# The first load of a rotary-embedding kernel in two pieces (16 and 112 partitions), and ScalarE copies of two PSUM banks each

## Chip, cores, metric

One core of a Trainium2 chip. The metric is the device time of one execution in microseconds (us). Most executions of one kernel agree within 0.3%; some, of any kernel, fall in a slower state and are left out of comparisons. Ratios below are the mean time of one kernel's fast runs over that of the other's fast runs of the same rounds, so they are not quite the ratio of the medians quoted beside them. Where some runs of a kernel fell in the slower state (the changed kernel, e1, e4, e5, e11), the median of its fast runs is given too; the ratio is what counts. Bytes and packet lengths come from one profiled fast run of each kernel.

## The reference

```python
# x: (8, 2048, 8, 64) f32; cos, sin: (2048, 32) f32
x1, x2 = x[..., :32], x[..., 32:]
out1 = x1 * cos - x2 * sin          # cos, sin broadcast over batch and heads
out2 = x1 * sin + x2 * cos
return np.concatenate([out1, out2], axis=-1)
```

It reads 33.6 MB of x and 0.5 MB of tables and writes 33.6 MB.

## The kernel before

The sequence lies on 128 partitions, 16 rows of it on each, so one batch is a tile of 128 x 8192 f32 (4 MB), loaded by the sync engine and stored by ScalarE's queue out of the same tile. GpSimd (POOL) makes the products with sin, VectorE (DVE) those with cos, and one of three ways adds them: "A" on VectorE; "B" on TensorE, which adds through an identity matrix into PSUM, from where ScalarE copies; "C" likewise, with both products on VectorE. Five units of 2048 columns go through TensorE, the first of batches 1 to 5.

```python
    o_pool = ctx.enter_context(tc.tile_pool(name="op", bufs=2, space=PSUM))
    ...
    def load(b):
        xt = xpool.tile([P, ROW], f32, tag="xt", name=f"xt{b}")
        for lo, n in spans([UNIT, UNIT, 2 * UNIT] if b == 0 else [ROW]):   # UNIT = 2048 columns
            keep(nc.sync.dma_start(out=xt[:, lo : lo + n], in_=xv[b, :, lo : lo + n]))
            if b == 0 and lo == 0:
                keep(nc.sync.dma_start(out=cos_sb, in_=cos_src))
                keep(nc.sync.dma_start(out=sin_sb, in_=sin_src))
    ...
        elif kind == "B":
            for j in range(n // C):                                        # C = 512, one bank
                o = o_pool.tile([P, C], f32, tag="o")
                cs = slice(j * C, (j + 1) * C)
                nc.tensor.matmul(o, eye, t1[:, cs], start=True, stop=False)
                nc.tensor.matmul(o, eye, t2[:, cs], start=False, stop=True)
                keep(nc.scalar.copy(xt[:, cs], o))
    ...
    def shares(b):                # columns of each store
        if b == 0:
            return [HD, 7 * HD, 2 * UNIT]                                  # HD = 512
        if b == last:
            return [2 * UNIT, UNIT, UNIT]
        return [ROW]
```

## Time and profile before

| | kernel before |
|---|---|
| time, median of 3 (then of 6) | 163.72 us (163.66) |
| span of the profiled run | 161.4 us |
| DMA share of the span | 98.2% |
| DVE, POOL, PE, ACT busy | 87%, 86%, 29%, 9% |

### The profile page before, as it was taken

Reading aid. Unit: us, or ns where it says so; the run is one execution under the profiler, and the core shown is the slowest. Engines: PE = TensorE matmul, PEld = TensorE weight load, DVE = VectorE, ACT = ScalarE, POOL = GpSimd, SP = SyncE. Lnnn points to the kernel's source line nnn. Section 1 sums busy time; section 2 is a strip of 40 time slices with the busy share of each in tenths; the row PEclk is TensorE's granted clock in tenths of the full one; section 3 lists DMA queues with packets and bytes.
Section 4 is the critical chain, followed back from the end, with each engine's and each line's share of the span. In section 5 each row is a group of like instructions: output and inputs, shape, how many; then the busy total and the mean of one; then the engine's idle time right before and its main releaser. Section 6 shows DMA issues by size and latency. Waiting matters only on the chain.

```text
span 161.4 us, 467 instructions
## 1 busy us (share of the span) xinstructions
PE 46.4 (29%) x80; PEld 18.5 (11%) x80; DVE 140.1 (87%) x66; ACT 14.4 (9%) x24; POOL 139.0 (86%) x70
## 2 busy tenths in 40 slices
PE   0000000498008960893029912980000000000000
PEld 0000000133003420340014401430000000000000
DVE  0468899999999999999999999999899998999900
ACT  3200000013000220032001210140000000000000
POOL 1299999999999899998996999998999979999200
PEclk9999999999955696599755985799555555555555
DMA  5999999899999999999999999999999999999995
GB/s 181 418 445 464 449 430 390 373 427 499 406 390 447 430 487 390 447 438 414 447 422 430 447 416 438 447 406 447 455 392 455 447 398 455 438 406 455 410 398 231
DMA packets 3458, 67.65 MB, mean 419 GB/s; under 512 B 384, under 2 KB 384, under 8 KB 768
## 3 DMA queue, kind: packets, MB, share of 16 engines
q1 hardware_dynamic: 1728, 34.08, 49.8%
q10 hardware_dynamic: 1728, 33.56, 48.4%
q14 instruction: 2, 0.02, 0.0%
HBM read 34.08 MB, written 33.55 MB: 419 GB/s over the span
## 4 chain that ended last, share of the span: by engine, by line
DMA 46%; DVE 37%; POOL 9%; issue 2%; SPq 1%; DVEq 0%; POOLq 0%; ACTq 0%
DMA xt<-in_x_dram 24%; DVE t L128 18%; DMA out_dram<-xt 18%; DVE xt L135 17%; POOL t L121 9%; DMA sin_sb<-in_sin_dram 3%; DVE t L145 1%; SPq L69 0%; SPq L67 0%; DVEq L135 0%; POOLq L121 0%; ACTq L74 0%
## 5 line engine op out<-in xcount | busy, mean ns | idle before, releaser
L121 POOL TENSOR_TENSOR t<-xt,sin_sb 128x1024 f32<-128x1024 f32 (+1 forms) x32 | 70.4, 2200 | 10.7 <-DMA sin_sb<-in_sin_dram 5.7
L128 DVE TENSOR_TENSOR t<-xt,cos_ps 128x2048 f32<-128x2048 f32 (+1 forms) x34 | 73.4, 2166 | 0.8
L121 POOL TENSOR_TENSOR t<-xt,nsin 128x1024 f32<-128x1024 f32 (+1 forms) x32 | 70.4, 2200 | 0.0
L135 DVE TENSOR_TENSOR xt<-t,t 128x2048 f32<-128x2048 f32 (+1 forms) x29 | 62.2, 2144 | 6.2 <-POOL t L121 3.7
L140 PE MATMUL o<-t,eye 128*128 128x512 f32 x24 | 17.1, 803 | 25.2 <-DVE t L128 25.2
L156 PE MATMUL o<-t,eye 128*128 128x512 f32 x16 | 10.9, 781 | 36.8 <-DVE t L128 36.8
L141 PE MATMUL o<-t,eye 128*128 128x512 f32 x24 | 15.0, 710 | 0.0
L142 ACT COPY xt<-o 128x512 f32<-128x512 f32 x12 | 7.0, 586 | 46.5 <-PE o L141 46.5
L140 PEld LDWEIGHTS o<-t,eye 128*128 128x128 f32 x24 | 5.6, 247 | 33.5 <-issue 33.5
L161 ACT COPY xt<-o 128x512 f32<-128x512 f32 x8 | 4.7, 586 | 42.6 <-PE o L157 42.6
L156 PEld LDWEIGHTS o<-t,eye 128*128 128x128 f32 x16 | 3.6, 247 | 41.7 <-POOL t L121 30.6
L141 PEld LDWEIGHTS o<-t,eye 128*128 128x128 f32 x24 | 5.9, 248 | 8.5 <-issue 8.5
L92 DVE COPY cos_ps<-cos_sb 128x512 f32<-128x512 f32 x1 | 0.7, 695 | 6.2 <-DMA cos_sb<-in_cos_dram 6.2
L157 PE MATMUL o<-t,neye 128*128 128x512 f32 x8 | 4.9, 714 | 0.2 <-DVE t L145 0.2
L145 DVE TENSOR_TENSOR t<-xt,sin_ps 128x2048 f32<-128x2048 f32 x2 | 4.6, 2279 | 0.0
L157 PE MATMUL o<-t,eye 128*128 128x512 f32 x8 | 4.1, 592 | 0.0
L157 PEld LDWEIGHTS o<-t,neye 128*128 128x128 f32 x8 | 1.8, 239 | 3.6 <-issue 3.6
L157 PEld LDWEIGHTS o<-t,eye 128*128 128x128 f32 x8 | 1.5, 190 | 1.9 <-issue 1.9
L89 ACT ACT_TABLE_LOAD x1 | 1.3, 1283 | 0.7 <-PEq L204 0.7
L89 ACT ACTIVATE nsin<-sin_sb 128x512 f32<-128x512 f32 x1 | 0.6, 629 | 4.9 <-DMA sin_sb<-in_sin_dram 4.9
L90 ACT COPY sin_ps<-sin_sb 128x512 f32<-128x512 f32 x1 | 0.6, 580 | 0.0
L79 POOL MEMSET eye<- 128x128 f32 x1 | 0.2, 205 | 0.3 <-POOLq L204 0.3
(6 smaller groups left out, 1.0 us busy)
## 6 DMA issues: line engine op xcount, KB each, us to landing
xt<-in_x_dram SPq DMA_DIRECT2D x7, 4096.0 KB, 38.9
out_dram<-xt ACTq DMA_DIRECT2D x6, 4096.0 KB, 28.3
out_dram<-xt ACTq DMA_DIRECT2D x2, 2048.0 KB, 18.9
xt<-in_x_dram SPq DMA_DIRECT2D x2, 1024.0 KB, 6.0
xt<-in_x_dram SPq DMA_DIRECT2D x1, 2048.0 KB, 11.5
out_dram<-xt ACTq DMA_DIRECT2D x2, 1024.0 KB, 8.7
out_dram<-xt ACTq DMA_DIRECT2D x1, 1792.0 KB, 20.4
cos_sb<-in_cos_dram SPq DMA_DIRECT2D x1, 256.0 KB, 5.0
```

The costliest lines, as they stand in the source:

```text
L89: keep(nc.scalar.mul(nsin, sin_sb, -1.0))
L92: keep(nc.vector.tensor_copy(cos_ps, cos_sb))
L121: nc.gpsimd.tensor_mul(out=t2u[:, :, u, :].rearrange("p (r h) d -> p r h d", h=H), in0=xu[:, :, 1 - u, :].rearrange("p (r h) d -> p r h d" ...
L128: nc.vector.tensor_mul(out=t1.rearrange("p (r k d) -> p r k d", r=nr, d=Dh), in0=xk, in1=rep(cos_ps[:, r0 : r0 + nr, :], 2 * H),)
L135: keep(nc.vector.tensor_add(out=xt, in0=t1, in1=t2))
L140: nc.tensor.matmul(o, eye, t1[:, cs], start=True, stop=False)
L141: nc.tensor.matmul(o, eye, t2[:, cs], start=False, stop=True)
L142: keep(nc.scalar.copy(xt[:, cs], o))
L145: nc.vector.tensor_mul(out=t2.rearrange("p (r k d) -> p r k d", r=nr, d=Dh), in0=xk, in1=rep(sin_ps[:, r0 : r0 + nr, :], 2 * H),)
L156: nc.tensor.matmul(o, eye, t1u[:, gs, u, :], start=True, stop=False)
L157: nc.tensor.matmul(o, eye if u else neye, t2u[:, gs, 1 - u, :], start=False, stop=True)
L161: nc.scalar.copy(xu[:, gs, u, :], o.rearrange("p (g d) -> p g d", d=Dh))
```

## The change

The intent: a small first load that gives each of the 16 DMA engines one row at once, so that all start early; and half as many ScalarE instructions. Cut to its core (the "C" branch is changed in the same way as "B"):

```diff
-    o_pool = ctx.enter_context(tc.tile_pool(name="op", bufs=2, space=PSUM))
+    o_pool = ctx.enter_context(tc.tile_pool(name="op", bufs=1, space=PSUM))
...
+    rows = {(0, 0): [slice(0, 16), slice(16, P)]}
...
-            keep(nc.sync.dma_start(out=xt[:, lo : lo + n], in_=xv[b, :, lo : lo + n]))
+            cs = slice(lo, lo + n)
+            for ps in rows.get((b, lo), [slice(0, P)]):
+                keep(nc.sync.dma_start(out=xt[ps, cs], in_=xv[b, ps, cs]))
...
-            for j in range(n // C):
-                o = o_pool.tile([P, C], f32, tag="o")
-                cs = slice(j * C, (j + 1) * C)
-                nc.tensor.matmul(o, eye, t1[:, cs], start=True, stop=False)
-                nc.tensor.matmul(o, eye, t2[:, cs], start=False, stop=True)
-                keep(nc.scalar.copy(xt[:, cs], o))
+            for j in range(n // (2 * C)):
+                o = o_pool.tile([P, 2 * C], f32, tag="o")
+                for k in range(2):
+                    cs = slice((2 * j + k) * C, (2 * j + k + 1) * C)
+                    oc = o[:, k * C : (k + 1) * C]
+                    nc.tensor.matmul(oc, eye, t1[:, cs], start=True, stop=False)
+                    nc.tensor.matmul(oc, eye, t2[:, cs], start=False, stop=True)
+                keep(nc.scalar.copy(xt[:, 2 * j * C : 2 * (j + 1) * C], o))
```

More of the change, by code (lines that the diff above doesn't have):

```diff
@@ L152, in rotate @@
             for u in range(2):
+                o = o_pool.tile([P, n // 2], f32, tag="o")
                 for j in range(n // 2 // C):
-                    o = o_pool.tile([P, C], f32, tag="o")
+                    oc = o[:, j * C : (j + 1) * C]
                     gs = slice(j * G, (j + 1) * G)
-                    nc.tensor.matmul(o, eye, t1u[:, gs, u, :], start=True, stop=False)
+                    nc.tensor.matmul(oc, eye, t1u[:, gs, u, :], start=True, stop=False)
                     nc.tensor.matmul(
-                        o, eye if u else neye, t2u[:, gs, 1 - u, :], start=False, stop=True
+                        oc, eye if u else neye, t2u[:, gs, 1 - u, :], start=False, stop=True
                     )
-                    keep(
-                        nc.scalar.copy(
-                            xu[:, gs, u, :], o.rearrange("p (g d) -> p g d", d=Dh)
-                        )
+                keep(
+                    nc.scalar.copy(
+                        xu[:, :, u, :], o.rearrange("p (g d) -> p g d", d=Dh)
                     )
+                )
     def pieces(b):
```

## The prediction

> **What bounds the kernel now.** I read the page first: engine shares, the DMA row over the 40 slices, the queues.
>
> ```profile
> PE 46.4 (29%) x80; PEld 18.5 (11%) x80; DVE 140.1 (87%) x66; ACT 14.4 (9%) x24; POOL 139.0 (86%) x70
> ...
> DMA  5999999899999999999999999999999999999995
> GB/s 181 418 445 464 449 430 390 373 427 499 406 390 447 430 487 390 447 438 414 447 422 430 447 416 438 447 406 447 455 392 455 447 398 455 438 406 455 410 398 231
> ...
> q1 hardware_dynamic: 1728, 34.08, 49.8%
> q10 hardware_dynamic: 1728, 33.56, 48.4%
> ```
>
> The two queues (loads, stores) together occupy 98.2% of the 16 DMA engines' span; DVE and POOL are near it with 87% and 86%, ScalarE is at 9%. So the first question is whether DMA or the DVE/POOL pair sets the end. Busy time by stretch (PE, PEld, DVE, ACT, POOL, then clock, DMA share, GB/s) shows where DMA is not full:
>
> ```profile
> 0.00:2.00 2.00, 0.00 (x0) 0.00 (x0) 0.00 (x0) 1.27 (x1) 0.70 (x6) 1.00 0.24 41
> 2.00:4.00 2.00, 0.00 (x0) 0.00 (x0) 0.00 (x0) 0.01 (x1) 0.00 (x0) 1.00 0.86 319
> 4.00:8.00 4.00, 0.00 (x0) 0.00 (x0) 1.76 (x2) 1.09 (x3) 0.97 (x1) 1.00 1.03 420
> 8.00:24.00 16.00, 0.00 (x0) 0.00 (x0) 13.44 (x9) 0.26 (x2) 16.00 (x10) 1.00 1.02 431
> ...
> 131.00:152.00 21.00, 0.00 (x0) 0.00 (x0) 19.79 (x11) 0.00 (x0) 18.60 (x10) 0.50 0.98 424
> 152.00:160.00 8.00, 0.00 (x0) 0.00 (x0) 1.23 (x1) 0.00 (x0) 0.00 (x0) 0.50 0.94 397
> ```
>
> Only the first 4 us are not full. By the packet records, 67.6 MB go between the first packet at 1.75 us and the end of the last at 160.25 us: 427 GB/s on average, 430 to 434 in nearly every stretch from 32 us on, whether it is load, store or a mixture. The time is therefore about 1.75 us of start, 158.5 us of full DMA, and 1.2 us until the program's end.
>
> Next, whether the end waits for DVE anyway. The last adds, and the issue of the last store (1 MB), stand in the order of time:
>
> ```profile
> 150.74 1.23 DVE L128 TENSOR_TENSOR t<-xt,cos_ps 128x1024 f32<-128x1024 f32 x1
> 152.07 1.23 DVE L135 TENSOR_TENSOR xt<-t,t 128x1024 f32<-128x1024 f32 x1
> ...
> 153.33 0.34 ACTq L74 DMA_DIRECT2D out_dram<-xt  x1
> ```
>
> That store lands at 160.6, 7.3 us later, although 1 MB is only 2.5 us of DMA: the store issued before it lands only at 158.2, so the last one starts moving at about 157.8. A store with a free queue would start about 1.0 us after its issue (the first load, below), at 154.3. So DVE could finish some 3 us later before it would delay the end. The chain of waits on the page names 37% DVE, but where it goes through the DMA (46%) it shows queueing; a shorter DVE would change nothing.
>
> **What the Trainium skill says.** "DMA: Bandwidth & Descriptors", section "Where 436 GB/s comes from", puts the ceiling of the 16 DMA engines' ports at 435.2 GB/s; the trace agrees, with 430 to 434. At that rate the 67.6 MB alone need 155.4 us (an estimate from that figure), so at most 3 us is to be had in the 158.5. The same page, "Latency and other measured facts", gives about 600 ns to the first byte of a DMA issued from sync; here the first issue ends at 1.11 us and the first packet starts at 1.75, 0.64 us later. Its section "Why a DMA increments its semaphore by 16 and not by 1" says that a copy runs on the largest number of engines up to 16 that divides its outermost size: 16 and 112 partitions both give 16, one row and seven rows per engine. "SBUF — State Buffer", section "Door 1: The DMA port swizzle", says that partitions 0 to 15 reach only 4 of the 16 memory-side ports and lists 104 GB/s for them at 1 MiB. No load of the kernel before has fewer than 128 partitions, so no run here shows that yet.
>
> **The change, part one: the split load.** The sync engine's issues now:
>
> ```profile
> 0.74 0.37 SPq L67 DMA_DIRECT2D xt<-in_x_dram  x1
> 1.16 0.43 SPq L69 DMA_DIRECT2D cos_sb<-in_cos_dram  x1
> 1.64 0.42 SPq L70 DMA_DIRECT2D sin_sb<-in_sin_dram  x1
> ```
>
> The spacing is 0.42 to 0.48 us. One more issue puts the cos, sin and all later loads some 0.45 us later in the sequencer. That alone costs nothing: cos would be issued at about 1.6 and queue behind 1 MB that moves until about 5 us. What can gain is the very first packets. By the packet records, the 16 engines' first packets (8 KB) start one after the other from 1.75 to 2.53 us, 2.03 on average, and take 0.39 to 1.09 us, against 0.309 us for an 8 KB packet later. If that stagger is the handing out of 8 rows to one engine after another, then 16 rows, one each, put all engines to work near 1.75; the 112 rows follow 0.42 us later, so the last engine gets them at about 2.53 + 0.42 - 0.1 = 2.85 us. That engine will by then have moved one packet; before, it had its first packet (0.58 us long) done at 3.11. Gain: about 0.25 us, and for the mean engine about 0.1 to 0.15 us. As DMA never idles again, it carries to the end nearly whole.
>
> Against it stands the port limit. 16 rows of 8 KB are 131 KB; at 104 GB/s (the skill's figure) they take 1.26 us, an estimate, where a full-width wave takes 0.31 us. Engines whose single row waits there until about 3.2 us would have moved one packet instead of the two and a half that they move now: a loss of up to 0.5 us on the slowest. In the 112-row load an engine's seven rows no longer lie on one port; I put collisions at 0 to 0.2 us. The sum of gain and loss runs from -0.25 to +0.7 us. I choose -0.1: first packets are slow now too (0.39 to 1.09 us), so part of the port wait lies inside that latency.
>
> **Part two: two banks per copy.** ScalarE's 20 copies of 512 columns take 0.586 us each, 11.7 us. Its two multiplications at the start (128 columns 0.299 us, 512 columns 0.629) give 0.86 ns per column, so 1024 columns should take 0.586 + 512 x 0.86 ns = 1.03 us; 10 of them are 10.3 us. ScalarE saves 1.4 us of work of which none is on a path. With one buffer of two banks in place of two of one bank, TensorE must wait for the copy between the halves of a unit, where it used to run on. Take the tightest case, the third batch:
>
> ```profile
> 57.44 0.59 ACT L142 COPY xt<-o 128x512 f32<-128x512 f32 x1 [1.13 <-PE o L141]
> 59.15 0.59 ACT L142 COPY xt<-o 128x512 f32<-128x512 f32 x1 [1.13 <-PE o L141]
> 63.05 0.34 ACTq L74 DMA_DIRECT2D out_dram<-xt  x1
> ```
>
> Copies come every 1.72 us, so one bank's matmuls take 1.72 us. The first double copy can start at 55.7 (where the second single copy started) and end at 56.75; two banks of matmuls end at about 60.3; the second double copy ends at about 61.4, against 59.74 now. The store is issued at 63.05, when DVE's last add is done: 1.6 us of slack left. Even with matmuls at the cold pace (0.86 us per pass, eight passes) the store slips under 2 us, and it would still queue behind the preceding store, which lands at 73.2. The buffers that TensorE holds longer (the operands t) are taken again later: the next batch's multiply into such a buffer starts at 62.88, and TensorE is done at 60.3. The built program keeps the same order on DVE, POOL, ScalarE and sync, with the waits on the same producers; TensorE loses half of its waits on ScalarE. Part two: 0.0 us.
>
> Sum: 163.72 - 0.1 + 0.0 = 163.6 us.
>
> **Rivals.** (1) The 16 rows crowd on four ports and the start is lost, not won: +0.3 to +0.7 us, 164.0 to 164.4. For it: the skill's table. Against it: it is 131 KB once. (2) The start gains more, because one slow engine carries its late start to the end: the last store's 16 completions are spread from 159.74 to 160.59, 0.85 us, about as wide as the stagger of 0.78 us at the start. If the stagger is what spreads the end, levelling it is worth up to 0.5 us: 163.2. (3) The serialised TensorE and ScalarE reach a path: it would need a slip of over 1.6 us and then a store queue that runs dry; the DMA row shows none, so 163.7 at most. (4) cos and sin land later, DVE starts later (now at 6.2 us) and takes the end: it needs 3 us, the extra issue is 0.45 us; 163.7.
>
> **Range and chances.** The three runs of before spread over 0.58 us, more than any single effect. I take -0.7 to +0.7 around the sum: 162.9 to 164.3. A change of 2% is 3.3 us, more than everything that the start and the end of the DMA stream hold together and could give (about 3 us) and four times the worst port loss. So within 2% has 0.98, and 0.01 for each side.
>
> **What would show it right or wrong.** In the changed kernel, DMA share 9 from the second slice on; the first packets of 16 engines all starting within about 0.2 us, near 1.75; their length tells the port question (0.4 to 0.9 us: no crowding; 1.2 us and over: rival 1). Ten ScalarE copies of 1.0 us; the third batch's last one ending near 61.4, before its store. DVE's last add within 0.5 us of 153.3. It would be wrong if DVE or POOL showed new waits for TensorE, if the stores were issued late enough for the DMA row to show a gap, or if the steady rate left 430 GB/s.

## More of the kernel before

What matters most for this change is the opening, in stretches of 2 us (length, PE, PEld, DVE, ACT, POOL busy with the number of instructions, then granted clock, DMA share, GB/s); kernel before:

```profile
2.00:4.00 2.00, 0.00 (x0) 0.00 (x0) 0.00 (x0) 0.01 (x1) 0.00 (x0) 1.00 0.86 319
4.00:6.00 2.00, 0.00 (x0) 0.00 (x0) 0.00 (x0) 0.00 (x0) 0.00 (x0) 1.00 0.97 385
6.00:8.00 2.00, 0.00 (x0) 0.00 (x0) 1.76 (x2) 1.09 (x3) 0.97 (x1) 1.00 1.09 455
8.00:10.00 2.00, 0.00 (x0) 0.00 (x0) 0.62 (x2) 0.26 (x2) 2.00 (x3) 1.00 1.07 455
```

DMA share and GB/s are two different things: the share counts the time that packets take, so an engine that waits inside a packet is "busy". Keep that in mind for the same lines after.

## The result, and the profile after

164.19 us median of 6 (164.03 to 169.16; fast runs 164.10) against 163.66 for the kernel before: ratio 1.0032, 95% interval 1.0017 to 1.0046. That is within 2%, and inside the range of the prediction, 0.1 us under its upper end; but the interval excludes 1, so the change costs about 0.5 us where the prediction had chosen a gain of 0.1.

The first profiled run fell in the slow state (169.16 us). There, 14 of the 16 completions of a late load came by 133.2 us and the last two at 137.5, some 4 us late, as if two DMA engines lagged; the last store ended in the same way, with 14 completions by 162.96 us and two at 166.48. The granted clock was no lower (0.768; 0.767 to 0.776 in this kernel's fast runs). The changed kernel was run again and profiled (e1 in the experiments, 164.17 us). Its page, answering to the prediction's first fence:

```profile
DMA  5999998989998999899899999999999999999994
GB/s 143 329 432 499 429 420 381 488 383 432 492 416 388 452 452 452 388 468 436 388 484 420 388 478 420 404 476 412 430 452 412 444 444 404 460 436 404 424 406 204
...
q1 hardware_dynamic: 1744, 34.08, 49.9%
q10 hardware_dynamic: 1728, 33.56, 48.1%
```

The queues hold 98.0% of the span, DMA is full from the second slice on, as before. Yet the first two slices moved 143 and 329 GB/s, where they moved 181 and 418. The opening of the same run:

```profile
2.00:4.00 2.00, 0.00 (x0) 0.00 (x0) 0.00 (x0) 0.01 (x1) 0.00 (x0) 1.00 0.92 234
4.00:6.00 2.00, 0.00 (x0) 0.00 (x0) 0.00 (x0) 0.00 (x0) 0.00 (x0) 1.00 0.99 284
6.00:8.00 2.00, 0.00 (x0) 0.00 (x0) 0.25 (x1) 0.00 (x0) 0.00 (x0) 1.00 1.07 372
8.00:10.00 2.00, 0.00 (x0) 0.00 (x0) 1.68 (x2) 1.35 (x3) 1.43 (x2) 1.00 1.12 467
```

Up to 6 us the share is as high as before, or higher, and the rate is a quarter lower; from 6 to 8 us it is still a fifth lower. The engines are at work all the time, on slower packets. After 8 us both run alike. The sync engine's issues and VectorE's first instruction, changed kernel:

```profile
0.74 0.83 SPq L70 DMA_DIRECT2D xt<-in_x_dram  x2
1.62 0.42 SPq L72 DMA_DIRECT2D cos_sb<-in_cos_dram  x1
...
7.75 0.69 DVE L95 COPY cos_ps<-cos_sb 128x512 f32<-128x512 f32 x1 [7.75 <-DMA cos_sb<-in_cos_dram]
```

cos is issued 0.46 us later than before and lands 1.55 us later (DVE starts at 7.75, where it started at 6.20), so 1.1 us of the delay is slower transfer. The end of the same run:

```profile
152.90 1.23 DVE L138 TENSOR_TENSOR xt<-t,t 128x1024 f32<-128x1024 f32 x1
...
154.15 0.34 ACTq L77 DMA_DIRECT2D out_dram<-xt  x1
```

VectorE ends 0.82 us later than before, not 1.55, because its waits for POOL and POOL's for x grew shorter. The last store is issued at 154.15 and lands at 161.48, while the store ahead of it lands only at 159.06: it still queues. DMA sets the end, as before. (The chain of waits on this page gives 75% to DVE and 4% to DMA, where the kernel before had 37% and 46%. It follows the last store back to its issue and from there to VectorE; how long that store then stood in its queue, it does not weigh. The two chains look like different bounds, and the bound is the same.)

### The profile page after: what moved, and what is told of

Same layout as the page of the kernel before. It is cut to its first block, busy times and chain, and to the rows that moved or that the text cites. A ratio compares the mean times of both kernels' runs of the same rounds, so it can differ in the third digit from the quotient of the medians.

```text
span 167.4 us, 461 instructions
## 1 busy us (share of the span) xinstructions
PE 48.8 (29%) x80; PEld 18.4 (11%) x80; DVE 140.1 (84%) x66; ACT 12.8 (8%) x14; POOL 139.0 (83%) x70
## 4 chain that ended last, share of the span: by engine, by line
DMA 47%; DVE 36%; POOL 8%; issue 2%; SPq 1%; DVEq 0%; POOLq 0%; ACTq 0%
DMA xt<-in_x_dram 25%; DMA out_dram<-xt 18%; DVE t L131 18%; DVE xt L138 17%; POOL t L124 8%; DMA sin_sb<-in_sin_dram 4%; DVE t L150 1%; SPq L70 0%; SPq L72 0%; DVEq L138 0%; POOLq L124 0%; ACTq L77 0%
## 5 line engine op out<-in xcount | busy, mean ns | idle before, releaser
L162 PE MATMUL o<-t,eye 128*128 128x512 f32 x16 | 11.9, 834 | 40.7 <-DVE t L131 38.5
L145 PE MATMUL o<-t,eye 128*128 128x512 f32 x24 | 16.7, 785 | 23.4 <-DVE t L131 19.9
L146 PE MATMUL o<-t,eye 128*128 128x512 f32 x24 | 14.9, 709 | 0.0
L147 ACT COPY xt<-o 128x1024 f32<-128x1024 f32 x6 | 6.1, 1012 | 45.7 <-PE o L146 45.7
L167 ACT COPY xt<-o 128x1024 f32<-128x1024 f32 x4 | 4.0, 1012 | 47.8 <-PE o L163 47.8
L163 PE MATMUL o<-t,neye 128*128 128x512 f32 x8 | 6.2, 863 | 0.2 <-DVE t L150 0.2
L163 PE MATMUL o<-t,eye 128*128 128x512 f32 x8 | 4.1, 592 | 0.0
```

The lines of the kernel that those rows point to most:

```text
L145: nc.tensor.matmul(oc, eye, t1[:, cs], start=True, stop=False)
L146: nc.tensor.matmul(oc, eye, t2[:, cs], start=False, stop=True)
L147: keep(nc.scalar.copy(xt[:, 2 * j * C : 2 * (j + 1) * C], o))
L162: nc.tensor.matmul(oc, eye, t1u[:, gs, u, :], start=True, stop=False)
L163: nc.tensor.matmul(oc, eye if u else neye, t2u[:, gs, 1 - u, :], start=False, stop=True)
L167: nc.scalar.copy(xu[:, :, u, :], o.rearrange("p (g d) -> p g d", d=Dh))
```

## The experiments

The tool for most of them is a count of bytes by time, from the start and length of every DMA packet in the trace (a packet is one row of a load on one DMA engine; its bytes are spread evenly over its length). MB moved since the start:

| kernel | 3 us | 4 us | 6 us | 8 us | 12 us | 24 us | 32 us | 64 us | last packet ends, us |
|---|---|---|---|---|---|---|---|---|---|
| before | 0.231 | 0.644 | 1.466 | 2.317 | 4.039 | 9.149 | 12.441 | 26.290 | 160.25 |
| changed (e1) | 0.215 | 0.498 | 1.087 | 1.796 | 3.496 | 8.666 | 12.123 | 25.969 | 161.14 |
| split only (e2) | 0.222 | 0.494 | 1.134 | 1.859 | 3.560 | 8.730 | 12.187 | 26.034 | 161.21 |
| banks only (e3) | 0.272 | 0.673 | 1.492 | 2.343 | 4.066 | 9.172 | 12.494 | 26.306 | 160.21 |
| column split (e4) | 0.225 | 0.565 | 1.361 | 2.191 | 3.912 | 9.040 | 12.339 | 26.177 | 160.77 |
| 112 first (e7) | 0.208 | 0.579 | 1.096 | 1.610 | 3.299 | 8.468 | 11.924 | 25.771 | 161.75 |
| 64 and 64 (e8) | 0.136 | 0.415 | 0.863 | 1.328 | 2.986 | 8.154 | 11.609 | 25.455 | 162.40 |

At 432 GB/s, 0.1 MB is 0.23 us. The changed kernel is 0.543 MB (1.26 us) behind at 12 us, and 0.318 MB (0.74 us) at 32 us: part is given back on the way. e1 and e2 have the same loads, so what lies between them, 0.15 us at 12 us, shows how far single traces differ.

Theories after the result. A: the shape of the loads costs; A1 in the 16 rows, A2 in the 112. B: one more DMA ahead of cos and sin costs, whatever its shape. C: the two-bank copies cost, since TensorE and ScalarE now take turns.

### e1 to e4: which part of the change

**e1_after_again**: the changed kernel, no edit.

> The changed kernel once more, for a profile of a fast run: the one at hand is of the slow state. All theories: 164.1 us, 0.3% over before. In the fast profile the opening should look as in the slow one: the 16 one-row packets take 0.3 to 0.5 us, the 112-row packets behind them 0.5 us and more, cos lands near 8.5 us instead of 6.2; and the end should be late by 0.5 to 0.8 us, with DMA full in between.

164.26 us median (fast runs 164.09 to 164.35) against 163.36; ratio 1.0036 (1.0010 to 1.0062). (The median of the four fast runs is 164.14.) The opening is slow in the expected way, though less than expected: cos is complete at 7.73 us, not 8.5, and the 8 KB packets between 3.5 and 5.5 us take 0.431 us. The last packet ends 0.89 us later.

**e2_split_only**: the kernel before with the `rows` lines of the diff alone.

> The split load alone, with the single-bank copies of before. Theory A (the shape of the 112-row load costs) and theory B (one more DMA ahead of cos and sin costs): all of the difference, +0.4 to +0.7 us over before. Theory C (the two-bank copies cost, through TensorE and ScalarE in turn): 0.0 us.

164.38 against 163.36; ratio 1.0052 (1.0029 to 1.0074). The split alone costs all of it.

**e3_banks_only**: the changed kernel with `rows = {}`.

> The two-bank copies alone, first load whole. Theories A and B: 0.0 us (within 0.1%). Theory C: +0.4 to +0.7 us. ScalarE's ten copies 1.01 us each in either case.

163.32 against 163.36; ratio 0.9990 (0.9966 to 1.0013). Theory C falls. ScalarE's copies in e1, by line:

```profile
L147 ACT COPY xt<-o 128x1024 f32<-128x1024 f32 x6 | 6.1, 1012 | 45.7 <-PE o L146 45.7
L167 ACT COPY xt<-o 128x1024 f32<-128x1024 f32 x4 | 4.0, 1012 | 48.1 <-PE o L163 48.1
```

And the tightest unit, the third batch's, in e3, where times compare with the kernel before:

```profile
55.05 1.01 ACT L147 COPY xt<-o 128x1024 f32<-128x1024 f32 x1 [11.74 <-PE o L146]
59.85 1.01 ACT L147 COPY xt<-o 128x1024 f32<-128x1024 f32 x1 [3.79 <-PE o L146]
63.06 0.34 ACTq L77 DMA_DIRECT2D out_dram<-xt  x1
```

The second double copy ends at 60.86, 1.1 us later than the last single copy did, and the store is issued at 63.06, as before at 63.05. There is 2.2 us of slack. TensorE does wait for ScalarE now (3.4 us in 3 waits in "B", 2.2 us in 2 in "C"), and apart from ScalarE, whose copies have the slack just shown, no engine waits for TensorE.

**e4_cols_first**: the same number of issues and bytes per piece as in the change, all of them at 128 partitions:

```diff
-            keep(nc.sync.dma_start(out=xt[:, lo : lo + n], in_=xv[b, :, lo : lo + n]))
+            parts = [(lo, 256), (lo + 256, n - 256)] if b == 0 and lo == 0 else [(lo, n)]
+            for at, m in parts:
+                keep(nc.sync.dma_start(out=xt[:, at : at + m], in_=xv[b, :, at : at + m]))
```

> The first 1 MB in two DMAs again, of the same 131 KB and 918 KB, but cut by columns: all 128 partitions in both (256 columns, then 1792). The order and number of issues are those of the changed kernel. Theory A (shape): no loss, 0.0 to +0.15 us, 8 KB-class packets at full rate by 3 us, cos landing at about 6.2 us. Theory B (one more DMA): the same +0.4 to +0.7 us as the changed kernel, cos landing near 8.5 us.

163.90 against 163.36 (fast runs 163.85); ratio 1.0017 (0.9987 to 1.0047), so by time alone it can't be told from either. The trace can: cos is complete at 6.71 us (6.18 before, 7.29 in e2, 7.73 in e1), packets between 3.5 and 5.5 us take 0.283 us for 7 KB, near the full rate (0.272), and at 12 us it is 0.29 us behind, where e2 is 1.11. Its opening:

```profile
4.00:6.00 2.00, 0.00 (x0) 0.00 (x0) 0.00 (x0) 0.00 (x0) 0.00 (x0) 1.00 0.98 378
```

So at 12 us a second DMA in front (theory B) has cost some 0.3 us and the shape (theory A) 0.8 us of the 1.1. At the end the two are closer, 0.52 and 0.96 us by the last packet, because e2 gets part back near 25 us (below) and e4 does not. Where the 0.29 us lie: the big load's packets start slowly whenever they start (19 of its 7 KB packets before 3 us took 0.756 us on average). Summed and divided by 16 engines, they take 0.66 us more than at full rate, against 0.51 for the first load before, and the 1 KB packets ahead take 0.10 more. Why a stream starts slowly is not shown.

### e5 to e8: which piece is the slow one

**e5_spare_cols** and **e6_spare_16rows**: the first load whole, and ahead of it a spare load of 131 KB into a buffer that gets its real data later. Results stay correct. e5's edit; e6 has `first[4][0:16, 0:UNIT]` and `xv[0, 0:16, 0:UNIT]` instead.

```diff
+    first = {b: xpool.tile([P, ROW], f32, tag="xt", name=f"xt{b}") for b in range(NBUF)}
...
+    keep(nc.sync.dma_start(out=first[4][:, 0:256], in_=xv[0, :, 0:256]))
     for b in range(NBUF):
         load(b)
```

> A spare load of 131 KB (128 partitions, 256 columns, into a buffer that is filled with its real data later) in front of the first load, which stays whole. It costs its bytes, 0.30 us at 432 GB/s, and a later start of the big load. From the column split (cos landed 6.7 us, +0.5 us at the end): cos at 6.9 to 7.0 us, time +0.4 to +0.7 us. 8 KB packets at 0.31 us from 3.5 us on. It is the base for the next run.

164.05 against 163.33 (fast runs 164.00); ratio 1.0042 (1.0024 to 1.0060).

> The same spare 131 KB, but as 16 partitions of 2048 columns; the real first load stays whole, 128 partitions. Theory A1 (the 16 rows crowd on few memory ports and hold up what is behind them): the spare load is complete at 3.1 to 3.7 us as in the changed kernel, and cos lands 0.6 to 1.0 us later than with the spare columns, at 7.6 to 8.0 us; the time is that much above it. Theory A2 (the 112-row load is the slow one, because seven rows per engine straddle the ports): no difference from the spare columns, cos at 6.9 to 7.0, and 8 KB packets at 0.31 us from 3.5 us on, where the changed kernel has 0.38 to 0.46.

164.19 against 163.33; ratio 1.0056 (1.0034 to 1.0078). cos complete at 6.80 us in e5 and 6.75 in e6. The opening of e5:

```profile
4.00:6.00 2.00, 0.00 (x0) 0.00 (x0) 0.00 (x0) 0.00 (x0) 0.00 (x0) 1.00 0.97 377
```

and of e6:

```profile
4.00:6.00 2.00, 0.00 (x0) 0.00 (x0) 0.00 (x0) 0.00 (x0) 0.00 (x0) 1.00 0.95 383
```

The 16 rows are complete at 3.05 to 3.54 us, the 131 KB in columns at 2.47 to 2.84: the 16 rows are slower by 0.6 us, in the direction of the port rule. But the load behind them runs at full rate (0.318 us per 8 KB packet between 3.5 and 5.5 us) and cos is not late. In this place A1 costs nothing that shows; A2 is left for the change. This rests on the packet lengths: by time alone neither run can be told from e2, since both move 131 KB more (0.30 us) and neither is spared the slow packets near 25 us (below), as e2 is.

**e7_split_112_first**: `rows = {(0, 0): [slice(16, P), slice(0, 16)]}`.

> The split in the other order, 112 rows and then 16. Theory A2: the 112-row packets are at 0.38 to 0.46 us here too, and the end is late by +0.5 to +0.8 us, as with the split of the change. Theory A1: the 112 rows run at 0.31 us a packet; the 16 rows slow what comes behind them (cos, sin), and the total is about the same, so the lengths decide, not the time.

164.90 against 163.33; ratio 1.0095 (1.0068 to 1.0122): slower than the change's order. 8 KB packets between 3.5 and 5.5 us take 0.475 us (0.431 in e1, 0.312 before):

```profile
4.00:6.00 2.00, 0.00 (x0) 0.00 (x0) 0.00 (x0) 0.00 (x0) 0.00 (x0) 1.00 1.02 242
```

If 112 rows only took as long as 128 do, a packet would take 0.357 us (an estimate, 8/7 of 0.312); so the smaller load took longer than the whole one. Then, behind the 16 rows, cos and sin's 2 KB packets take 0.208 us on average between 5.5 and 7 us, against 0.086 before. So both pieces cost here: the 112 rows are slow, and the 16 rows hold up what follows, probably because now they come inside a running stream (e9 bears on this). I had expected the same total as with the split of the change; it was 0.5 us more.

**e8_split_64_64**: `rows = {(0, 0): [slice(0, 64), slice(64, P)]}`.

> The first 1 MB as partitions 0 to 63 and then 64 to 127. If what counts is how many memory ports a load's partitions reach (theory A in either form, from the skill's table: 64 partitions reach 8 of 16 ports, 196 GB/s), 1 MB takes about 5 us instead of 2.5: 8 KB packets of about 0.6 us, cos lands at 8.0 to 8.7 us, and the time is +1.0 to +2.5 us. If ports do not matter and only the extra issue does: cos at 6.7 us, +0.3 to +0.5 us as with the column split.

165.48 against 163.33; ratio 1.0135 (1.0109 to 1.0161); cos complete at 8.82 us. The opening:

```profile
4.00:6.00 2.00, 0.00 (x0) 0.00 (x0) 0.00 (x0) 0.00 (x0) 0.00 (x0) 1.00 0.96 213
6.00:8.00 2.00, 0.00 (x0) 0.00 (x0) 0.00 (x0) 0.00 (x0) 0.00 (x0) 1.00 0.94 213
```

Half the rate, and 8 KB packets of 0.589 us instead of 0.312, with all 16 DMA engines at work (share 0.96). That fits the port table of the Trainium skill ("SBUF — State Buffer", "Door 1: The DMA port swizzle"): 64 partitions reach 8 of 16 ports, with an asymptote of 218 GB/s.

### e9: the split in a second, bigger load

**e9_split_two_batches**: e2 with `(1, 0): [slice(0, 16), slice(16, P)]` as well: 16 rows and 112 rows of 32 KB.

> The split load alone, and the second batch's 4 MB load split in the same way, 16 rows of 32 KB and then 112. If the straddling of the 112 rows slows the stream by its bytes (8 KB packets took 0.42 us on average against 0.309, a factor of 1.35), seven 32 KB packets per engine take 1.64 us instead of 1.21: +3.0 us over the split of the first 1 MB alone, about 167.3 us. If the loss belongs to the start-up of the stream alone, the second split costs nothing beyond its issue: 164.4 us.

172.55 against 163.44; ratio 1.0565 (1.0538 to 1.0593), the only kernel here that is clearly slower by more than 2%. Kernel e9, stretches around that load:

```profile
12.00:20.00 8.00, 0.00 (x0) 0.00 (x0) 7.00 (x5) 0.00 (x0) 8.00 (x5) 1.00 1.13 267
20.00:32.00 12.00, 0.00 (x0) 0.00 (x0) 9.53 (x5) 0.00 (x0) 7.14 (x4) 1.00 1.01 273
```

The same in the kernel before:

```profile
12.00:20.00 8.00, 0.00 (x0) 0.00 (x0) 6.99 (x5) 0.00 (x0) 8.00 (x4) 1.00 1.04 447
20.00:32.00 12.00, 1.39 (x2) 0.50 (x2) 11.76 (x6) 0.00 (x0) 12.00 (x6) 1.00 1.01 413
```

The 16 one-row packets take 3.83 us each (3.15 to 4.36), against 1.21 us: 524 KB in 3.83 us is 137 GB/s, and by their completions (19.55 to 21.09 us, begun at 14.6) less than that. The packets behind them take 2.16 us between 17.5 and 22.3 us, 1.88 between 22.3 and 33. Worked out: 2.6 us lost on the first packet, seven times 0.8 us on the others, 8.2 us together; the time is 8.2 us over e2's (172.55 - 164.38). The profiled run, the slowest of e9's four, is 9.2 us over e2's (173.5 - 164.3), so about 1 us of it is not in that sum. My expectation was 167.3: the direction was right and the size too small, because here the 16 rows, of 32 KB each and in the middle of a full stream, lose 2.6 us, and the 112 rows are slowed by 1.6 to 1.8 instead of 1.35. The loss does not belong to the start-up alone: it grew with the bytes, and the first 1 MB was the cheaper of the two places tried.

### e10 to e12: what gives part of the loss back, and a try for a better version

Of the 1.26 us that the changed kernel is behind at 12 us, 0.52 are given back by 32 us, most of it near 25 us. The page of DMA between 22 and 26 us, kernel before:

```profile
DMA packets 114, 1.41 MB, mean 352 GB/s; under 512 B 32, under 2 KB 32, under 8 KB 64
```

and e1:

```profile
DMA packets 128, 1.67 MB, mean 418 GB/s; under 512 B 31, under 2 KB 31, under 8 KB 80
```

In the kernel before, 29 of the 32 KB load packets near the border of the second and the third load take up to 1.7 us instead of 1.21, 0.54 us per engine; e3, e4, e5 and e6 lose 0.35 to 0.55 us there too, e1, e2, e7 and e8 nothing. Three tries for the reason:

**e10_spare_1024cols**: e5 with 1024 spare columns instead of 256.

> A spare load of 128 partitions and 1024 columns (524 KB) ahead of everything, all shapes at full width: the stream comes 1.2 us late, as with the split, but at full speed. It is to tell why kernels with a 112-row or 64-row load lose nothing at the border of the second and third load (near 25 us), where all full-width kernels lose 0.35 to 0.55 us. If it is the time at which the border comes: no slow 32 KB packets there, end +0.7 us. If it is the shape of the first loads: 0.4 to 0.5 us of slow packets there as before, end +1.2 us, 164.6.

165.10 against 163.44; ratio 1.0102 (1.0083 to 1.0121). Slow packets at the border: 0.49 us. A later start alone does not remove them; the shape of the first load has to do with it.

**e11_first_store_whole**: `return [2 * UNIT, 2 * UNIT]` for the stores of batch 0.

> The kernel before, with the first batch stored in two halves instead of 256 KB, 1.75 MB and 2 MB. In the kernel before, the 2 KB packets of the small store end just when the second load ends, and the slow packets come there. If that meeting makes them: none near 25 us, and 0.3 to 0.5 us less than before (162.9 to 163.1), which would be the best version. If the border of the loads alone makes them: 163.4 +- 0.2.

163.66 against 163.44 (fast runs 163.56); ratio 1.0016 (0.9997 to 1.0035). The slow packets are still there, at 20 to 23 us, and cost 0.83 us. They are no longer at the border: all of them belong to the second load, and the third load's first packet starts at 25.2 us.

**e12_load1_halves**: batch 1 loaded as `[2 * UNIT] * 2`.

> The kernel before, with the second batch loaded as two halves of 2 MB (16 KB packets) instead of 4 MB in one. A try for a version that beats both: every full-width kernel loses 0.35 to 0.85 us in slow 32 KB packets at the border of the second and third load, while the border of the first and second, from 16 KB to 32 KB packets, shows none. If the slow packets need 32 KB packets on both sides of the border: none near 25 us, and 162.9 to 163.1 us. If they come with the third load whatever precedes it: 163.4 +- 0.2.

163.67 against 163.37; ratio 1.0016 (1.0002 to 1.0030). Slow packets (16 KB now, in the second half of the second batch) from 20.8 to 25.1 us, 0.7 us; the third load's first packet starts only at 26.7 us. So neither the border nor the third load is needed for them, which neither expectation had allowed for, though the times came near those given for the border (163.4). What makes them stays open; so does how a first load in 112 or 64 rows goes with their absence. No version tried beats the kernel before; e3 equals it.

## Why the prediction was right, and where it was not

- **The bound**: right. DMA fills the span in every kernel; a late opening carries to the end, less what the border near 25 us gives back. The page, the two ends and e3 agree.
- **Part two costs 0.0 us**: right (e3: 0.9990). A double copy takes 1.012 us (1.03 predicted); the third batch's last ends at 60.86 (61.4 predicted), before its store.
- **The split's gain of 0.25 us on the slowest engine**: the first packets did come a little closer together, and were shorter (0.43 us on average, which by the prediction's own test meant no crowding). The traces name no DMA engine, so the prediction's last first packet at 2.53 us is a guess at which packets share one; what can be counted is that the first sixteen packets start by 2.36 us before and by 2.17 after, not within 0.2 us of 1.75. The gain did not reach the stream. The term left out: the big load has a slow start of its own. e4, where every piece has all 128 partitions, is 0.29 us behind at 12 us instead of ahead.
- **"In the 112-row load an engine's seven rows no longer lie on one port; I put collisions at 0 to 0.2 us"**: this is the step that failed, in its size. The prediction gives no source for where the rows lie, and no run shows it. Seven packets of 0.431 us instead of 0.312 are 0.83 us; together with cos and sin's packets behind them the shape cost 0.8 to 1.0 us by 12 us.
- **The port wait of the 16 rows, up to 0.5 us**: no difference that could be measured in that place (e6 against e5: 0.2 us in medians of fast runs, intervals overlapping; cos not later). It lies inside the start-up, as the prediction thought. In the middle of the stream it is real (e9: 3.83 us instead of 1.21).
- **"I choose -0.1" out of -0.25 to +0.7**: wrong sign. Measured +0.5 us at first, +0.6 in e1 (both by the ratio of fast runs). That the range held, by 0.1 us, is partly luck: rival 1, "the 16 rows crowd on four ports and the start is lost" (164.0 to 164.4), had the right size, with the wrong piece named.
- **Rival 2** (levelling the stagger is worth 0.5 us) did not show: the last store's completions spread over 1.06 us in e1, 0.85 before. **Rival 4** (a later DVE takes the end): its delay was 0.82 us at the end, over the 0.45 assumed and the 0.5 allowed for, and hidden in the queue.
- The prediction read the start as a question of when packets begin. The loss was in how long they took, which only the packet lengths or the GB/s beside the share could show.

That the 112 rows are slow because an engine's rows straddle ports is inferred: 112 partitions touch all 16 ports, so a count of ports does not explain it. The runs show a rate for each shape, not which engine wrote to which port. Rivals were not tried: seven rows per engine instead of a power of two, or a start at partition 16 instead of 0.

## What to carry to other kernels

Cutting a load by partitions is not free, even when each piece has a row for every DMA engine: here 128 rows ran at 0.31 us per 8 KB, 112 rows at 0.43, 64 rows at 0.59. If a small first piece is wanted, cut columns and keep all 128 partitions, and expect no gain even then: e4, cut in that way, was not faster (1.0017, 0.9987 to 1.0047) and had moved less by 12 us. And read the GB/s beside the DMA share: between 4 and 6 us a share of 0.99 stood beside 284 GB/s with the split, and 0.97 beside 385 without it.

## What the Trainium skill lacked or had wrong

- "SBUF — State Buffer", "Door 1: The DMA port swizzle": its table holds for 64 partitions (213 GB/s in e8, asymptote 218 there). It lists no range that reaches all ports unevenly: 112 partitions (16 to 127) ran at 0.431 us per 8 KB packet against 0.312 for 128, and at 1.9 to 2.2 us per 32 KB packet against 1.21.
- The same section gives 104 GB/s for partitions 0 to 15. As 16 packets of 8 KB at the start of a stream they delayed nothing behind them that shows (e6); as 16 packets of 32 KB in a full stream they took 3.83 us (137 GB/s by packet length). The page doesn't say that the cost depends on the place in a stream; these two runs differ in the size of the packets too.
- "DMA: Bandwidth & Descriptors", "Why a DMA increments its semaphore by 16 and not by 1": engine counts of 16 for 16, 64 and 112 partitions are consistent with the DMA shares seen (0.92 and over from 2 to 8 us in e1 and e8), but the page warns of no loss of rate at a full count, and 213 to 303 GB/s were seen.
- "DMA: Bandwidth & Descriptors", "Latency and other measured facts": the 600 ns to the first byte agree (0.64 us). No page has the slow first packets of a stream: the first sixteen 8 KB packets of the kernel before took 0.34 to 1.09 us instead of 0.31, and the slow start cost about 0.5 us per engine in all.
- No page has the slow load packets between 20 and 28 us: 0.35 to 0.83 us per engine in every kernel here that loads the first 1 MB of x with 128 partitions in each piece, none in those that load it in 112 or 64 rows (e9 can't be read there).
